# A hybrid attention, recurrence and MLP block on one core: the stretch from the output projection to the MLP, with token halves, a first half scaled by ScalarE and an order written out

## Chip, cores and metric

The kernel runs on one core of one Trainium2 chip. The metric is the device time in microseconds of one execution, as the median of several runs. A core has five engines with a queue each: PE (TensorE, matrix products), DVE (VectorE), ACT (ScalarE), POOL (GpSimd) and SP (SyncE, which here only issues DMAs). Each takes its own instructions strictly in the order of the built program and waits where a semaphore tells it to.

## What is computed

One layer on x of 1024 tokens by 1024 channels, in float32. Two branches (attention and a recurrence) give `merged`; the part that the change touches comes behind them:

```python
h = x.astype(f32) + merged @ w_out[layer].astype(f32)

hn = rmsnorm(h, norm2_g[layer])
a = jnp.square(jax.nn.relu(hn @ w_ff1[layer].astype(f32)))
h = h + a @ w_ff2[layer].astype(f32)
...
return rmsnorm(h, final_g).astype(x.dtype)
```

with `rmsnorm(x, g)` = x / sqrt(mean(x^2) + eps) * g, 1024 by 1024 for `w_out`, 1024 by 4096 for `w_ff1`.

## The kernel before

**Products.** A float32 product is made of three: each operand is split into a high part (a rounded copy, made by ACT, `hi_copy`, L142 in the profile) and a low part (the rest, a subtraction by DVE, `lo_sub`, L147). `three` issues high times high, low times high and high times low (L121). A "product" here has four steps of depth 128, so twelve matmuls of up to 512 columns into one PSUM bank. There are eight banks.

**Seven products instead of eight.** The projection, the MLP's first matrix (up) and its second (down) are each cut in two by two blocks and computed by a scheme of seven block products over sums of blocks. The names W, X, Y, V, Z are the banks of these products, and `LANDS` or the code of `out_start`, `out_rest`, `out_last` say with which sign each is added to which quadrant of the result.

**Projection** (`out_start`, `out_rest`, `out_last`). The token rows come in eight blocks of 128, `hres[0]` to `hres[7]`, called h in the profile. Blocks 0 to 3 are one half of the rows of the scheme and 4 to 7 the other. `out_start` computes W and X for four rows each; `out_rest(0..3)` computes Y from m1 and w1 (bank pwY), which two adds on DVE put into the right halves of h[tb] and h[4+tb]; `out_rest(4..7)` computes V from mb and w21 (pwV) for the left half of h[4+tb]; `out_last` computes Z from m4 and w22 (pwZ) for the right half of h[4+tb].

**Norm** (`norm2_token`). When a token block is complete, ACT squares it and sums along the row (L1451), POOL makes the factor in two small steps (L230 mean and eps, L233 power of -0.5, called n_ss and n_y), DVE multiplies block, factor and norm gain g2b (L1462, hn), and POOL issues a DMA that writes the block to DRAM (hd, L1467), from where the end of the kernel reads it back.

**Turning and forms** (`Quads`). PE turns hn by 128 by 128 transposes (L124) into banks hnt; ACT copies them to SBUF as hnq (L329). Quads holds two "halves" q = 0, 1 of the tokens for the MLP's scheme: before, q is the parity of the block (even and odd ones), so that each pair of blocks gives one transposed part of both. The operands of the seven up products are: 1 and 2, the q = 0 half itself; 6, 5, 7, 4, 3 sums of halves (made by DVE in `sums`, L347). Each form is split into sqh and sql.

**MLP up** (`UpPair`). 16 pairs, each of twice 128 columns of `w_ff1`; a pair has products 1 and 2 (bank pW), 6, 7, 4 (pX) and 5, 3 (pY), with its weights split as b11h/l, whiu/wlou and t0, t1 (sums of weight blocks). The first two pairs run ahead: their products 1 and 2 are cut here into two calls of 256 columns, the first of them while the last tokens are still normed. `mlp_up` then goes through the other pairs, with pair 2's first product inside it.

**MLP down and end** (`mlp_down`). Products pm over 32 steps; at the end blocks are normed once more and written out, even ones during the last group of steps, odd ones at its end.

**What sets the order.** A scheduler places the instructions of an engine by their dependencies and the order of the code. Where `after` adds a dependency without a semaphore, the order is fixed; `in_turn` does this for all of ACT's or DVE's instructions that go through it while `turns["on"]` is set. In the stretch of the change it is off before; `last_evac` orders some of ACT's.

Of the kernel before, what the change touches and what calls it, by code (L numbers as in the profile page):

```python
# [19 lines left out]
P = 128  # L20
# [19 lines left out]
def kernel(  # L40
# [94 lines left out]
    def in_turn(engine, ins):  # L135
        if turns["on"]:
            after(ins, turns[engine])
            turns[engine] = ins
        return ins

# [152 lines left out]
    class Quads:  # L293
# [3 lines left out]
        def __init__(self):  # L297
            self.raw, self.hl, self.s1 = {}, {}, []

# [4 lines left out]
        def fill(self, pr, src, name):  # L304


            banks = []
            for kp in range(KT // 2):
                if pr == 0:
                    for q in range(2):  # L310
                        self.raw[q, kp] = slot(f"{name}q{q}{kp}")
                pb = bank(f"{name}t{pr}{kp}")
                open_block("fill")
                for q in range(2):
                    for j in range(2):
                        kt, b = 2 * kp + j, 2 * q + j
                        transpose(
                            pb[:, b * P : (b + 1) * P],
                            src[2 * pr + q][:, kt * P : (kt + 1) * P],
                        )  # L320
                banks.append(pb)
                self.leave(pr, 0, kp, pb)
                self.split(1 + kp // 2, kp % 2, self.raw[0, kp], pr, 1)
            for kp in range(KT // 2):
                self.leave(pr, 1, kp, banks[kp])

        def leave(self, pr, q, kp, pb):
            last_evac[0] = after(
                nc.scalar.copy(  # L329
                    self.part(self.raw[q, kp], pr, 1),  # L330
                    pb[:, q * 256 : (q + 1) * 256].rearrange("p (k t) -> p k t", k=2),
                ),
                last_evac[0],
            )

        def split(self, i, kp, src, pr=0, n=4):
            if (i, kp) not in self.hl:
                self.hl[i, kp] = tuple(slot(f"sq{n_}{i}{kp}", F32R) for n_ in "hl")
            h, l = (self.part(t, pr, n) for t in self.hl[i, kp])
            self.last_lo = hi_lo(h, l, self.part(src, pr, n))  # L340

        def sums(self, pr, n, first=True, then=True):
            r = self.raw

            def tt(out, a, b, op):
                after(
                    nc.vector.tensor_tensor(  # L347
                        out=self.part(out, pr, n),
                        in0=self.part(a, pr, n),
                        in1=self.part(b, pr, n),  # L350
                        op=op,
                    ),
                    self.last_lo,
                )

            for kp in range(2):
                if pr == 0 and first:
                    self.s1.append(slot(f"sq1{kp}"))
                if first:
                    tt(self.s1[kp], r[1, kp], r[1, kp + 2], ALU.add)  # L360
                    tt(r[1, kp], r[0, kp], r[1, kp], ALU.subtract)
                    tt(r[0, kp], self.s1[kp], r[0, kp], ALU.subtract)
            for kp in range(2):
                if then:
                    tt(r[0, kp + 2], r[0, kp + 2], r[0, kp], ALU.subtract)

        def sum_form(self, i):
# [8 lines left out]
            for kp in range(2):  # L376
                self.split(i, kp, src[kp])

        def form(self, i, k, c0=0, n=512):
            h, l = self.hl[i, k // 2]  # L380
            c = (k % 2) * 512 + c0
            return h[:, c : c + n], l[:, c : c + n]
# [1056 lines left out]
    hsrc, hd = {}, {}  # L1439
# [3 lines left out]
    def norm2_token(tb):  # L1443
        hsrc[tb] = slot(f"hn{tb}")
        parts = 2 if tb == NT - 1 else 1
        cuts = [slice(i * D // parts, (i + 1) * D // parts) for i in range(parts)]
        sums = []
        for i, cs in enumerate(cuts):
            ssq = small.tile([P, 1], F32, tag="ssq1", name=f"n2_{tb}_ss{i}", bufs=4)
            after(  # L1450
                nc.scalar.activation(  # L1451
                    hsrc[tb][:, cs], hres[tb][:, cs], AF.Square, accum_out=ssq
                ),
                last_evac[0],
            )
# [3 lines left out]
        r = inv_rms(sums[0], 1, 1.0 / D, f"n2_{tb}")  # L1459
        yield  # L1460
        for cs in cuts:
            nc.vector.scalar_tensor_tensor(  # L1462
                out=hsrc[tb][:, cs], in0=hres[tb][:, cs], scalar=r, in1=g2b[0][:, cs],
                op0=ALU.mult, op1=ALU.mult,
            )
        hd[tb] = dram(f"hd{tb}", [P, D])
        nc.gpsimd.dma_start(hd[tb], hres[tb])  # L1467
# [7 lines left out]

    def out_operands(w=(), m=(), last=None):

        for n in w:
            src = tw[int(n)] if len(n) == 1 else out_block(int(n[0]) - 1, int(n[1]) - 1)
            out_form[n] = out_unit(n, src)  # L1480
            out_form[n].split()
        for n in m:
            merged[n] = []
            for kp in range(2):
                r = slot(f"m{n}r{kp}")
                h, l = slot(f"m{n}h{kp}", F32R), slot(f"m{n}l{kp}", F32R)
# [656 lines left out]
```

## Time and profile before

| What | us |
|---|---|
| median of 3 runs | 1462.3 |
| lowest and highest | 1461.54, 1463.45 |
| the profiled execution | 1462.87 |
| its span, first to last instruction | 1460.8 |

The stretch of the change lies between about 789 and 897 us of the span: the last twelve products of the projection, the norms and transposes, and the first products of the MLP. In rows of the timeline the columns are start, length, engine, line, operation, output<-inputs and shape; in brackets stands how long the engine sat idle before, and what ended that. A matmul's length (0.39 us at 512 columns) overlaps the next one's; they start 0.23 us apart.

### The profile page before, as it was taken

Reading aid. Unit: us, or ns where it says so; the run is one execution under the profiler, and the core shown is the slowest. Engines: PE = TensorE matmul, PEld = TensorE weight load, DVE = VectorE, ACT = ScalarE, POOL = GpSimd, SP = SyncE. Lnnn points to the kernel's source line nnn. Section 1 sums busy time; section 2 is a strip of 40 time slices with the busy share of each in tenths; the row PEclk is TensorE's granted clock in tenths of the full one; section 3 lists DMA queues with packets and bytes.
Section 4 is the critical chain, followed back from the end, with each engine's and each line's share of the span. In section 5 each row is a group of like instructions: output and inputs, shape, how many; then the busy total and the mean of one; then the engine's idle time right before and its main releaser. Section 6 shows DMA issues by size and latency. Waiting matters only on the chain.

```text
span 1460.8 us, 20051 instructions
## 1 busy us (share of the span) xinstructions
PE 1437.6 (98%) x7490; PEld 1224.0 (84%) x7490; DVE 1105.9 (76%) x1591; ACT 671.5 (46%) x1180; POOL 132.9 (9%) x319
## 2 busy tenths in 40 slices
PE   8999999999999999999999899999999999999997
PEld 8889988988898888888887788888888888888886
DVE  6699898698757787887777898666666757768765
ACT  7566666552323334423355464444444533523333
POOL 3021111000000012100011200000000000000041
PEclk9999999999999999999999999999999999999999
DMA  7143255001213349655489213444445975676734
GB/s 209 34 120 88 60 107 109 16 29 53 86 30 101 78 155 249 216 187 190 149 281 314 100 51 130 159 151 151 158 159 178 354 262 185 249 279 242 280 103 171
DMA packets 157736, 227.30 MB, mean 156 GB/s; under 512 B 25308, under 2 KB 92936, under 8 KB 157640
## 3 DMA queue, kind: packets, MB, share of 16 engines
q1 hardware_dynamic: 142664, 184.07, 37.2%
q0 software_dynamic: 11376, 35.40, 9.4%
q10 hardware_dynamic: 3600, 6.56, 1.2%
q8 instruction: 59, 0.97, 0.3%
q14 instruction: 37, 0.30, 0.1%
HBM read 163.34 MB, written 62.65 MB: 155 GB/s over the span
## 4 chain that ended last, share of the span: by engine, by line
PE 92%; DVE 4%; POOL 1%; issue 1%; DMA 1%; ACT 1%; SPq 0%; POOLq 0%; DVEq 0%; ACTq 0%
PE pm L121 18%; PE pX L121 9%; PE pY L121 6%; PE pW L121 6%; PE pjqk L121 6%; PE pjv L121 3%; PE pga L121 3%; PE pjq L121 3%; PE pys L121 3%; PE pyh L121 3%; PE gY L121 3%; PE gX L121 3%; PE pji L121 3%; PE pjf L121 3%; PE pjg L121 3%; PE po L121 3%
## 5 line engine op out<-in xcount | busy, mean ns | idle before, releaser
L142 ACT CAST whid<-w 128x1024 fp32r<-128x1024 f32 x31 | 32.6, 1053 | 153.6 <-PE pm L121 88.9
L679 DVE TENSOR_TENSOR_SCAN rm<-rm,bits 128x511 f32<-128x511 f32 (+7 forms) x72 | 87.2, 1219 | 14.4 <-ACT rm L657 12.8
L121 PE MATMUL pm<-wlod,sh 128*128 128x512 f32 x248 | 96.6, 390 | 1.0 <-DVE wlod L147 1.0
L121 PE MATMUL pm<-whid,sl 128*128 128x512 f32 x248 | 96.5, 389 | 0.0
L121 PE MATMUL pm<-whid,sh 128*128 128x512 f32 x248 | 96.5, 389 | 0.0
L147 DVE TENSOR_TENSOR wlod<-w,whid 128x1024 fp32r<-128x1024 f32 x31 | 37.9, 1223 | 58.3 <-ACT whid L142 58.3
L121 PE MATMUL pm<-th,sl 128*128 128x512 f32 x200 | 77.8, 389 | 0.0
L121 PE MATMUL pm<-tl,sh 128*128 128x512 f32 x200 | 77.8, 389 | 0.0
L121 PE MATMUL pm<-th,sh 128*128 128x512 f32 x200 | 77.8, 389 | 0.0
L147 DVE TENSOR_TENSOR sl<-sa,sh 128x1024 fp32r<-128x1024 f32 x56 | 68.2, 1219 | 1.4 <-ACT sh L142 1.4
L142 ACT CAST wTh<-pw 128x128 fp32r<-128x128 f32 (+3 forms) x96 | 44.4, 487 | 50.1 <-PE pw L124 45.2
L142 ACT CAST sh<-sa 128x1024 fp32r<-128x1024 f32 x56 | 57.2, 1046 | 12.1 <-DMA sa<-ad 12.1
L147 DVE TENSOR_TENSOR wTl<-pw,wTh 128x512 fp32r<-128x512 f32 (+3 forms) x96 | 50.7, 547 | 9.9 <-ACT wTh L142 5.4
L121 PEld LDWEIGHTS pm<-wlod,sh 128*128 128x128 f32 x248 | 46.5, 188 | 11.1 <-DVE wlod L147 1.4
L1809 POOL TENSOR_SCALAR fss<-fss 128x1 f32<-128x1 f32 x8 | 4.5, 561 | 563.0 <-ACT fsc L1804 562.5
L121 PEld LDWEIGHTS pm<-whid,sh 128*128 128x128 f32 x248 | 46.6, 188 | 9.8
L121 PEld LDWEIGHTS pm<-whid,sl 128*128 128x128 f32 x248 | 46.5, 187 | 9.6
L155 DVE TENSOR_TENSOR bt<-bt,rm 128x511 f32<-128x511 f32 (+7 forms) x72 | 49.0, 686 | 4.5 <-ACT bt L660 0.3
L657 ACT ACTIVATE rm<-z 128x511 f32<-128x511 f32 (+6 forms) x96 | 47.6, 503 | 5.2 <-DVE bt L155 1.9
L121 PE MATMUL pX<-sql,t1h 128*128 128x512 f32 x128 | 49.8, 389 | 0.0
L121 PE MATMUL pX<-sqh,t1h 128*128 128x512 f32 x128 | 49.8, 389 | 0.0
L121 PE MATMUL pX<-sqh,t1l 128*128 128x512 f32 x128 | 49.8, 389 | 0.0
(920 smaller groups left out, 4602.6 us busy)
## 6 DMA issues: line engine op xcount, KB each, us to landing
w<-in_w_ff_dram SPq DMA_DIRECT2D x72, 512.0 KB, 4.6
sa<-ad SPq DMA_DIRECT2D x56, 512.0 KB, 6.5
ad<-a SPq DMA_DIRECT2D x32, 256.0 KB, 4.1
ad<-s SPq DMA_DIRECT2D x16, 512.0 KB, 3.6
tw<-in_w_out_dram POOLq DMA_DIRECT2D x6, 1024.0 KB, 7.4
x<-in_x_dram SPq DMA_DIRECT2D x8, 512.0 KB, 9.5
xnl<-xnh POOLq DMA_DIRECT2D x8, 512.0 KB, 9.9
pr<-pd SPq DMA_DIRECT2D x8, 512.0 KB, 6.2
```

Of the source, the lines that this page charges most:

```text
L121: return pe(nc.tensor.matmul(*a, **k))
L142: return in_turn("act", nc.scalar.copy(dst, src))
L147: nc.vector.tensor_tensor(out=dst, in0=src, in1=hi.bitcast(F32), op=ALU.subtract),
L155: return nc.vector.tensor_tensor(out=out, in0=a, in1=b, op=ALU.mult)
L657: nc.scalar.activation(rm[:, s0 + c0 - 1 : s0 + m - 1], z[:, c0:m], AF.Sigmoid, scale=-0.125)
L679: sc = nc.vector.tensor_tensor_scan(out=rr, data0=rr, data1=bits[:, 1024 - nk + a : 1024 - nk + b][:, ::-1], initial=rm[:, b : b + 1] if i ...
L1809: nc.gpsimd.tensor_scalar(out=ssq, in0=ssq, scalar1=1.0 / D, scalar2=EPS, op0=ALU.mult, op1=ALU.add)
```

## The change

1. *Halves alike.* The MLP's two token halves are now blocks 0 to 3 and 4 to 7, as in the projection, instead of even and odd ones. The transposes of a half's pair of blocks fill four banks of their own (`turned`, `leave`), and `land`, `finish_tokens` and the last norms use the new numbers.
2. *First half scaled by ScalarE.* For blocks 0 to 3 ACT multiplies by the row's factor, and the norm gain, which after the transpose belongs to a partition, is put in when ACT copies out of PSUM. Blocks 4 to 7 stay with DVE.
3. *Last product onto the bank of the sum.* Y is added to h[tb] only; Z is accumulated onto Y's bank, and one add puts both into h[4+tb].
4. *First products among the norms.* Products 1 and 2 of the first two pairs are issued at the full 512 columns between the transposes of blocks 4 to 7, and product 1 of pair 2 behind them.
5. *Order written out.* From the first Y to the first `x7`, ACT's and DVE's instructions follow the code; loads of mb, w22 and m4 are separated from their splits; hd is issued behind the factors.

```diff
+        def leave(self, q, pr):
+            for kp, pb in self.banks.items():
+                if q == 0:
+                    for j in range(2):
+                        g = prm[:, G2 + 2 * kp + j : G2 + 2 * kp + j + 1]
+                        dst = self.part(self.raw[0, kp], 2 * pr, 2)[:, j]
+                        bs = slice(2 * j * P, 2 * (j + 1) * P)
+                        act(nc.scalar.activation(dst, pb[:, bs], AF.Identity, scale=g))
+                else:
+                    src = pb.rearrange("p (k t) -> p k t", k=2)
+                    act(nc.scalar.copy(self.part(self.raw[1, kp], 2 * pr, 2), src))
...
+    def norm2_scale(tb, parts=1):
+        n = D // parts
+        for i in range(parts):
+            cs = slice(i * n, (i + 1) * n)
+            if tb < 4:
+                scaled[tb] = act(
+                    nc.scalar.activation(
+                        hsrc[tb][:, cs], hres[tb][:, cs], AF.Identity, scale=rms[tb]
+                    )
+                )
+                continue
...
-            for h in (hres[tb][:, right], hres[4 + tb][:, right]):
-                turn_dve(add(h, h, oY[tb]))
...
+    def out_z(tb):
+        out_product(oY[tb], "4", "22", tb, False)
         h = hres[4 + tb][:, right]
-        turn_dve(add(h, h, Z))
+        dve(add(h, h, oY[tb]))
...
-            h = hres[2 * tb + int(q[0]) - 1]
+            h = hres[4 * (int(q[0]) - 1) + tb]
...
+    turns.update(on=True, act=None, dve=None)
     for tb in range(4):
+        out_y(tb)
+        if tb == 1:
+            merged_split("b")
+        norm2_sums(tb)
         if tb > 0:
+            norm2_scale(tb - 1)
+    first[0].sums()
+    out_v(0)
+    add_v(0)
+    out_v(1)
+    norm2_scale(3)
     for tb in range(4):
+        leave_h(tb, scaled[3])
+    merged_load("4")
+    add_v(1)
+    hn.turned(0, 0, hsrc, "hn")
+    hn.leave(0, 0)
+    out_operands(["22"])
+    out_v(2)
+    add_v(2)
+    merged_split("4")
+    out_v(3)
+    add_v(3)
+    hn.turned(0, 1, hsrc, "hn")
+    hn.leave(0, 1)
+    hn.first_hi(0)
+    hn.first_lo()
+    first[1].sums()
+    hn.first_hi(1)
+    out_z(0)
+    norm2_sums(4)
+    hn.first_lo(2)
+    out_z(1)
+    norm2_sums(5)
+    norm2_scale(4)
+    hn.first_lo(2)
+    leave_h(4, scaled[4])
     pairs[2].load()
+    out_z(2)
+    norm2_sums(6)
+    norm2_scale(5)
+    leave_h(5, scaled[5])
+    out_z(3)
+    norm2_sums(7, 2)
+    norm2_scale(6)
+    leave_h(6, scaled[6])
+    first[0].w1()
     for u in first:
+        u.sum_hi(1)
+        u.sum_lo(1)
+    norm2_scale(7, 2)
+    leave_h(7, scaled[7])
+    hn.turned(1, 0, hsrc, "hn")
+    hn.leave(1, 0)
+    for kp in range(2):
+        hn.sums(0, 2, kp)
+    first[0].w2()
+    pairs[2].split_first()
+    first[1].w1()
+    hn.turned(1, 1, hsrc, "hn")
...
+    first[1].w2()
+    pairs[2].w1()
```

The built program shows three places. On POOL, at the norms of the first blocks (hd are the blocks on their way to DRAM, n_ss and n_y the two steps of a factor), before:

```order
L1467 DMA hd_7908<-h_7487 128x1024
L1467 DMA hd_7932<-h_7488 128x1024
L1467 DMA hd_7956<-h_7489 128x1024
L1467 DMA hd_7973<-h_7490 128x1024
L230 TENSOR_SCALAR n_0_ss_7881<-n_0_ss_7881 128x1
L233 TENSOR_TENSOR n_0_y<-n_0_ss_7881,expo 128x1
```

and with the change, from the third block on:

```order
L236 TENSOR_SCALAR n_2_ss_7913<-n_2_ss_7913 128x1
L239 TENSOR_TENSOR n_2_y<-n_2_ss_7913,expo 128x1
L236 TENSOR_SCALAR n_3_ss_7934<-n_3_ss_7934 128x1
L239 TENSOR_TENSOR n_3_y<-n_3_ss_7934,expo 128x1
L1491 DMA hd_7972<-h_7487 128x1024
L1491 DMA hd_7974<-h_7488 128x1024
```

The four issues of hd moved from ahead of the four factors to behind them.

On ACT, from the first square sum to the first copy out of a transposed bank, before:

```order
L1451 ACTIVATE hn_7880,n_0_ss_7881<-h_7487 128x1024
L1451 ACTIVATE hn_7901,n_1_ss_7902<-h_7488 128x1024
L1451 ACTIVATE hn_7925,n_2_ss_7926<-h_7489 128x1024
L1451 ACTIVATE hn_7949,n_3_ss_7950<-h_7490 128x1024
L142 CAST m4h_7980<-m4r_7979 128x1024
L142 CAST m4h_7986<-m4r_7985 128x1024
L329 COPY hnq_8023<-hnt_8025 128x2x128
```

and with the change (mbh is the high part of mb; n_0_y as an input marks a scaling by the factor):

```order
L1465 ACTIVATE hn_7867,n_0_ss_7868<-h_7487 128x1024
L148 CAST mbh_7798<-mbr_7797 128x1024
L148 CAST mbh_7802<-mbr_7801 128x1024
L1465 ACTIVATE hn_7891,n_1_ss_7892<-h_7488 128x1024
L1477 ACTIVATE hn_7867<-h_7487,n_0_y 128x1024
L1465 ACTIVATE hn_7912,n_2_ss_7913<-h_7489 128x1024
L1477 ACTIVATE hn_7891<-h_7488,n_1_y 128x1024
L1465 ACTIVATE hn_7933,n_3_ss_7934<-h_7490 128x1024
L1477 ACTIVATE hn_7912<-h_7489,n_2_y 128x1024
L1477 ACTIVATE hn_7933<-h_7490,n_3_y 128x1024
L333 ACTIVATE hnq_7989<-hnt_7990,prm 128x256 x2
```

The four scalings came to ACT, each one square sum behind its own; mb's split moved in among them, and m4's behind the first copies.

On DVE, at the last product of the projection and the norms of blocks 4 to 6, before:

```order
L1072 TENSOR_TENSOR h_7491<-h_7491,pwZ_8135 128x512
L1072 TENSOR_TENSOR h_7492<-h_7492,pwZ_8158 128x512
L1462 SCALAR_TENSOR_TENSOR hn_8149<-h_7491,n_4_y,g2b 128x1024
L1462 SCALAR_TENSOR_TENSOR hn_8172<-h_7492,n_5_y,g2b 128x1024
L1072 TENSOR_TENSOR h_7493<-h_7493,pwZ_8181 128x512
L147 TENSOR_TENSOR sql_8032<-hnq_8023,sqh_8031 128x2x128
L1462 SCALAR_TENSOR_TENSOR hn_8195<-h_7493,n_6_y,g2b 128x1024
```

and with the change:

```order
L1087 TENSOR_TENSOR h_7491<-h_7491,pwY_7853 128x512
L153 TENSOR_TENSOR sql_8090<-hnq_7989,sqh_8089 128x2x256
L153 TENSOR_TENSOR sql_8093<-hnq_7995,sqh_8092 128x2x256
L1087 TENSOR_TENSOR h_7492<-h_7492,pwY_7873 128x512
L1483 SCALAR_TENSOR_TENSOR hn_8126<-h_7491,n_4_y,g2b 128x1024
L153 TENSOR_TENSOR sql_8096<-hnq_8001,sqh_8095 128x2x256
L153 TENSOR_TENSOR sql_8099<-hnq_8007,sqh_8098 128x2x256
L1087 TENSOR_TENSOR h_7493<-h_7493,pwY_7898 128x512
L1483 SCALAR_TENSOR_TENSOR hn_8147<-h_7492,n_5_y,g2b 128x1024
L1087 TENSOR_TENSOR h_7494<-h_7494,pwY_7919 128x512
L1483 SCALAR_TENSOR_TENSOR hn_8175<-h_7493,n_6_y,g2b 128x1024
```

The low parts of the first half, now 512 wide, stand between an add and the scaling of that block, and the scaling of block 4 stands behind the add of block 5.

More of the change, by code (lines that the diff above doesn't have):

```diff
@@ L298, in __init__ @@
             self.raw, self.hl, self.s1 = {}, {}, []
+            self.later = deque()
         @staticmethod
@@ L320, in fill @@
                         )
[L321 to L333, printed above, removed]
-            )
@@ L336, in split @@
[L336 to L342, printed above, removed]
-            r = self.raw
[L345 to L365, printed above, removed]
@@ L2061 @@
-    for tb in range(4, NT):
-        out_last(tb - 4)
-        if tb == NT - 1:
-            for u in first:
-                last_evac[0] = after(u.sum_hi(1), last_evac[0])
-            first[0].w1(0, 256)
-        side = norm2_token(tb)
-        next(side)
-        if tb == NT - 1:
-            hn.sums(2, 1, then=False)
-        if tb == 6:
-            hn.fill(2, hsrc, "hn")
-        for _ in side:
-            pass
-    pairs[2].load()
-    first[1].w1(0, 256)
-    first[0].w2(0, 256)
-    first[0].sum_lo(1)
@@ L2087 @@
-    hn.sums(3, 1, then=False)
-    hn.sum_form(6)
-    after(first[1].sum_lo(1), hn.last_lo)
+        u.sum_hi(0)
+        u.sum_lo(0)
+    for kp in range(2):
+        hn.next_sum(kp)
     for u in first:
         u.x6()
-    first[0].sum_split(0)
-    hn.sum_form(5)
-    first[1].sum_hi(0)
-    after(first[1].sum_lo(0), hn.last_lo)
+    hn.sum_form(7)
     for u in first:
         u.y5()
-    hn.sum_form(7)
+    for kp in range(2):
+        hn.last_sum(kp)
+    hn.sum_form(4)
+    turns["on"] = False
@@ L2099 @@
     for u in first:
         u.x7()
-    hn.sums(2, 2, first=False)
-    hn.sum_form(4)
     pairs[2].split()
```

294 lines of the change are left out of this document (158 added, 136 removed).

## The prediction

> **What bounds the kernel now.** The page first. PE is busy almost throughout, so time can only come from where PE waits or runs slow.
>
> ```profile
> span 1460.8 us, 20051 instructions
> PE 1437.6 (98%) x7490; PEld 1224.0 (84%) x7490; DVE 1105.9 (76%) x1591; ACT 671.5 (46%) x1180; POOL 132.9 (9%) x319
> ```
>
> The chain in order of time finds the place. Its columns are start, length, work.
>
> ```profile
> 789.24 10.89 PE pwY L121 x48
> 809.17 4.87 DVE hn L1462 x4
> 853.58 5.47 PE pX L121 x24
> 894.41 2.72 PE pW L121 x12
> 897.13 2.95 PE pX L121 x13
> ```
>
> A product is twelve 512-wide matmuls: 2.72 us (the pW row). From the first pwY (789.24) to pair 3's first pX (897.13) pass 107.9 us, and the chain leaves PE for DVE, POOL and ACT between. From 853.58 on it is PE again, sixteen products in 43.55 us, which is 16 x 2.72 with no loss. The PE timeline shows the waits in brackets, with what ended them:
>
> ```profile
> 803.24 0.51 PE L121 MATMUL pwV<-wout21h,mbl 128*128 128x512 f32 x1 [1.30 <-DVE mbl L147]
> 810.51 0.44 PE L124 MATMUL hnt<-ident,hn 128*128 128x128 f32 x2 [0.59 <-DVE hn L1462]
> 811.70 1.75 PE L124 MATMUL hnt<-ident,hn 128*128 128x128 f32 x14 [0.76 <-DVE hn L1462]
> 816.03 2.26 PE L124 MATMUL hnt<-ident,hn 128*128 128x128 f32 x16
> 829.10 0.41 PE L124 MATMUL hnt<-ident,hn 128*128 128x128 f32 x2 [2.60 <-DVE hn L1462]
> 831.01 3.25 PE L124 MATMUL hnt<-ident,hn 128*128 128x128 f32 x14 [1.50 <-DVE hn L1462]
> 838.15 0.28 PE L121 MATMUL pW<-sqh,b11h 128*128 128x256 f32 x1
> 838.27 0.28 PE L121 MATMUL pW<-sql,b11h 128*128 128x256 f32 x1
> 845.34 1.75 PE L124 MATMUL hnt<-ident,hn 128*128 128x128 f32 x14 [1.77 <-DVE hn L1462]
> ```
>
> The waits sum to 8.5 us. The other loss is the clock, third number from the end in the view by windows:
>
> ```profile
> core 0: us, PE busy (x) PEld busy (x) DVE busy (x) ACT busy (x) POOL busy (x), PEclk, DMA share, GB/s
> 810.00:815.00 5.00, 3.73 (x24) 3.21 (x25) 5.00 (x5) 2.64 (x8) 0.00 (x0) 1.00 0.00 0
> 830.00:835.00 5.00, 3.99 (x17) 3.79 (x18) 2.61 (x4) 3.26 (x10) 1.60 (x3) 0.51 0.55 187
> 835.00:840.00 5.00, 5.00 (x27) 4.35 (x26) 3.31 (x9) 3.38 (x8) 0.61 (x1) 0.81 0.97 285
> 818.00:898.00 80.00, 74.13 (x376) 63.38 (x375) 67.99 (x109) 47.90 (x90) 8.80 (x13) 0.96 0.28 102
> ```
>
> 0.49 x 3.99 + 0.19 x 5.00 = 2.9 us lost to the clock, right after the 2.60 and 1.50 us waits. Now the whole stretch: PE's own work is 12 products of the projection (32.6), 96 half-wide matmuls at 838.27 - 838.15 = 0.12 (11.5), 64 transposes at about 0.12 (sixteen start within 2.26 - 0.27; 7.7) and 43.5 behind 853.58: 95.3. So 107.9 - 95.3 = 12.6 are lost: 8.5 waits, 2.9 clock, 1.2 crumbs.
>
> **The change, part by part.** *Full width.* The first two pairs' pW go from 96 half-wide to 48 full matmuls, 10.9 us for 11.5: -0.6. Pair 2's first product only moves ahead. PE's work to the same point is then 32 x 2.72 + 7.7 = 94.7, so the most that this stretch can give is 107.9 - 94.7 = **13.2 us**.
>
> *Norms of the first half.* Why hn came at 809.17, although the square sums of the first tokens were ready long before, the timelines of ACT and POOL show:
>
> ```profile
> 795.93 0.19 ACT L1451 ACTIVATION_READ_ACCUMULATOR hn<-h 128x1 f32 x1
> 801.14 0.53 POOL L1467 DMA_DIRECT2D hd<-h  x1 [1.23 <-DVE h L1072]
> 801.74 0.35 POOL L230 TENSOR_SCALAR n_ss<-n_ss 128x1 f32<-128x1 f32 x1
> 802.18 1.43 POOL L233 TENSOR_TENSOR n_y<-n_ss,expo 128x1 f32<-128x1 f32 x1
> 805.05 0.56 POOL L233 TENSOR_TENSOR n_y<-n_ss,expo 128x1 f32<-128x1 f32 x1
> ```
>
> A square sum was there at 796.1; POOL's four issues of hd stood ahead of its two small steps, the last of them waiting for a DVE add until 801.14. Now they stand behind, so a norm costs its sum (1.06 + 0.19), two POOL steps (0.35 + 1.43 here) and a scaling. ScalarE's scaling from a per-token factor has no row in this width; the nearest:
>
> ```profile
> L1451 ACT ACTIVATE hn<-h 128x1024 f32<-128x1024 f32 x7 | 7.4, 1055 | 6.9 <-DVE h L1072 6.9
> L1823 ACT ACTIVATE y<-hb,fr x4: 722/722/725, 1447.7 to 1455.9; 128x512 f32<-128x512 f32 x4
> ```
>
> The full-width Square takes 1.06, two half-wide scalings from such a factor 1.44; I take 1.15, near the row of the same width. Four DVE scalings (4.87) and four of the eight adds of pwY (4 x 0.60) leave DVE. The scaling adds a wait on ACT for POOL: behind it stand the next token's square sum and later the first evacuation, which PE's third pwV waits for through its bank. Token 1's chain ends about 5.4 + 0.6 + 1.2 + 1.8 + 1.1, and 1 behind other ACT work, = 11 us after pwY begins; PE comes to its transposes after six products, 16.3. So 5 us of slack, and the 0.59 and 0.76 go. The 1.30 goes as well: b's low parts are due at 10.9, and with ACT's casts at 4.5 to 6.4 they are done near 9, since DVE has only eleven 512-wide and six 1024-wide instructions in this quarter, 13.4 us of 25.6 at the prices below.
>
> *The last operands.* The splits of w22 and m4 now follow the first evacuation on ACT: eight scaled 256-wide copies, then four casts. Nearest rows: scaled copies of the first norm, and plain ones here.
>
> ```profile
> L280 ACT ACTIVATE xnh<-xnt,prm x24: 465/502/731, 9.6 to 36.1; 128x256 fp32r<-128x256 f32 x16, 128x512 fp32r<-128x512 f32 x8
> L329 ACT COPY hnq<-hnt 128x256 f32<-128x256 f32 x32 | 10.6, 385 | 17.7 <-PE hnt L124 17.7
> ```
>
> Less 0.1 of overlap, 0.28 to 0.4 each: 2.3 to 3.2; I take 2.9. Then four casts as wide as that Square, 4 x 0.95, and DVE's 1.14 for the last low part: m4's low is whole about 9.6 after the transposes begin; the last product starts at 9.3 and needs that part 1.8 later. The four banks of pwY stay taken, so the third pwV waits for the first bank of transposes: two copies, done about 1.4 after the block began, which lasts 1.9. Zero for both, at most 1 us together. The loads of w22 and m4 keep their place in SP's queue; hd's four writes, later now, meet the idle DMA of the 810 row.
>
> *Second half.* Four norms remain on DVE, each waiting for POOL, and PE has a pair's first product (2.72) between the transposes. That covers most of the 2.60 + 1.50 + 1.77; with them goes the slow clock (2.9).
>
> *What is late next: DVE.* PE no longer gives it time. Count its order from the last pwV add to the low half of pair 3's sums, which pX of pair 3 waits for: 58 adds or splits 512 wide, 23 of 1024, 3 scalings of 1024 and 2 of 512. Prices are start to start:
>
> ```profile
> 894.45 0.69 DVE L1072 TENSOR_TENSOR a<-p,pX 128x512 f32<-128x512 f32 x1
> 895.17 0.69 DVE L1072 TENSOR_TENSOR a<-a,pY 128x512 f32<-128x512 f32 x1
> 895.77 1.22 DVE L147 TENSOR_TENSOR t1l<-w_3r,t1h 128x1024 fp32r<-128x1024 f32 x1
> ```
>
> The second starts 0.72 after the first, which it needs, the third 0.60 after the second: 0.69 less 0.09. So 0.60 and, of 1.22, 1.14; scalings 1.2 (809.17) and about 0.7. So 34.8 + 26.2 + 3.6 + 1.4 = 66.0 (before, 68.0 in 818 to 898, the windows row). PE has in that stretch 24 products and 32 transposes, 69.2. DVE may wait 3.2 us in all; what it waits beyond, PE waits. Before it waited:
>
> ```profile
> DVE hn L1462 <- POOL n_y L233: 4.6, 4, 2.4
> DVE sql L147 <- ACT sqh L142: 3.1, 3, 1.9
> DVE h L1072 <- PE pwZ L121: 1.7, 1, 1.7
> DVE t1l L147 <- ACT t1h L1648: 1.1, 1, 1.1
> DVE u L1072 <- PE pY L121: 0.8, 1, 0.8
> DVE wlou L147 <- ACT whiu L142: 0.3, 1, 0.3
> ```
>
> That is 11.6. Low end: only ten dependent neighbours at 0.12, 1.2, so nothing is given back. High end: all 11.6 again and these 1.2: 9.6 back. I take 8.3, nearer the upper end, since these norms still wait for POOL and the new order still puts low parts behind ACT's copies: 8.3 - 3.2 = **5.1 back**, as many short PE waits among the norms and up to pair 3.
>
> Beyond pair 3 the loops are the same, and so is the tail, where tokens only change names. Sum: 13.2 - 5.1 = 8.1. The profiled span 1460.8 becomes 1452.7; that execution took 1462.87, so 2.1 lie outside: 1454.8. It stood 0.57 above the median, hence **1454.2** for the median.
>
> **The rivals.**
> *A: DVE keeps up.* With waits of 1.2 to 3.2 in that stretch nothing comes back: all 13.2 are gained, 1449.1. The plain 0.56 step at 805.05 speaks for it, the 1.43 against.
> *B: the second half's norms stay late.* If one POOL answer slips by 2 us, as the 2.60 did, the transposes of tokens 4 and 5 wait, the clock drops again (2.9), and DVE's waits go to the upper end: 13.2 - 9.6 = 3.6 gained, the clock's loss lying in the same time: 1458.7. For it: POOL still issues hd between the norms. Against: DVE and PE have other work in between.
> *C: the relief is worth nothing.* What was taken from DVE early doesn't help if its later order decides alone; with 14 us of waits there, more than any row adds up to, 10.8 come back and 2.4 are left: 1459.9.
> *D: slower, through POOL.* Its small steps stretch while DVE works, once very far:
>
> ```profile
> 1419.98 4.65 POOL L1813 TENSOR_SCALAR fss<-fss,fss 128x1 f32<-128x1 f32 x1
> ```
>
> DVE waits in a written order, so if one step of each of four norms took 4.65 for 0.35, that is 17.2 us later: 1454.2 + 17.2 = 1471. It decides from 2 us per norm on. Against it: DVE itself stands still while it waits, which leaves POOL alone; 4.6 was the sum of four before. The Trainium skill, "SBUF — State Buffer", Who interferes with whom, has a VectorE instruction with two SBUF inputs contend with GpSimd reads. The trace agrees: 0.56 beside an add from PSUM, 1.43 beside a split.
>
> *E: transposes slow the clock.* PE now runs four blocks of sixteen, two of them beside norms. If one cost the clock as the 830 rows show, 2.9 us, the time is 1457.1. Between 809.9 and 813.4 PE ran transposes alone, with 1.35 of waits, and the 810 row has a clock of 1.00; the new blocks last 1.9 and a wait, so I give it little. The Trainium skill, "TensorE: Matmul & The Clock Gate", Part 4: PE-mode transpose, says that transposes do not count as busy in the same way, and by it E would be the likelier; the 810 row speaks against that, the 830 row fits either.
>
> **How the numbers follow.** Forecast 0.61, A 0.10, B 0.14, C 0.08, D 0.04, E 0.03. A measurement of this kernel tells about 0.2% (2.9 us) from no change. Faster are the forecast, A, B and E, 0.88; same C, 0.08; slower D, 0.04. The range goes from nearly all of A (0.4 back) to the upper end of what DVE gives back (9.6): 1449.5 to 1458.7. Outside lie part of A, C and D, under 0.2.
>
> **What would show it.** Right: one granted clock of 1.00 from 790 to 900; no PE wait for mbl or hn over 1 us; POOL's n_y of token 0 within 4 us of pwY's first add; afterwards short PE waits ended by DVE's sql, t1l or a, about 5 us in sum, with DVE over 90% busy. Wrong: a half clock behind the last product (B), PE waits on m4l, or DVE waits for n_y above 2 us each (D); no PE waits at all would be A.

## The result and the profile after

| | before | with the change |
|---|---|---|
| median, us | 1462.1 (4 runs, 1461.54 to 1463.45) | 1455.0 (4 runs, 1454.49 to 1455.19) |
| ratio to before, 95% interval | | 0.995 [0.9932, 0.9967] |
| the profiled execution, us | 1462.87 | 1454.49 |
| its span, us | 1460.8 | 1452.7 |

The change makes the kernel 0.5% shorter, and the interval does not reach 1. The page of the changed kernel: PE is at 99% in place of 98%, over a span 8.1 us shorter.

```profile
span 1452.7 us, 19895 instructions
PE 1436.7 (99%) x7442; PEld 1219.9 (84%) x7442; DVE 1096.7 (75%) x1557; ACT 675.6 (47%) x1166; POOL 125.2 (9%) x319
```

Where the 8.1 us lie is seen by three marks of the PE timeline: the first matmul of the first pwY, the first of pair 3's pX and the first of pm, with which the MLP's second matrix begins.

```profile
789.26 0.39 PE L121 MATMUL pwY<-wout1h,m1h 128*128 128x512 f32 x1
...
888.32 0.50 PE L121 MATMUL pX<-sqh,t1h 128*128 128x512 f32 x1
...
1139.89 0.39 PE L121 MATMUL pm<-whid,sh 128*128 128x512 f32 x1
```

The kernel before has the same marks here:

```profile
789.08 0.39 PE L121 MATMUL pwY<-wout1h,m1h 128*128 128x512 f32 x1
...
896.97 0.39 PE L121 MATMUL pX<-sqh,t1h 128*128 128x512 f32 x1
...
1147.20 0.39 PE L121 MATMUL pm<-whid,sh 128*128 128x512 f32 x1
```

From the first mark to the second 107.89 us became 99.06 (-8.8); to the third, 358.12 became 350.63 (-7.5): 1.3 us are lost again in and behind the pX of pair 3. Another 0.8 came off behind the third mark, and 0.2 were lost ahead of the first; together the 8.1. These are all waits of PE of 0.2 us or more from 785 to 905 us, in the timeline of the changed kernel:

```profile
829.37 1.86 PE L124 MATMUL hnt<-ident,hn 128*128 128x128 f32 x15 [0.64 <-DVE hn L1483]
856.21 0.50 PE L121 MATMUL pX<-sql,t0h 128*128 128x512 f32 x1 [0.23 <-DVE sql L153]
862.57 0.47 PE L121 MATMUL pX<-sqh,t1h 128*128 128x512 f32 x1 [0.85 <-DVE a L1087]
874.74 0.49 PE L121 MATMUL pX<-sqh,t1l 128*128 128x512 f32 x1 [0.52 <-DVE t1l L153]
889.68 0.50 PE L121 MATMUL pX<-sqh,t1l 128*128 128x512 f32 x1 [0.64 <-DVE t1l L153]
```

The waits of 1.30 for mbl, of 2.60, 1.50 and 1.77 for hn are gone; five short ones are left, 2.9 us in sum, and four of them stand behind the norms. The windows show the clock (third number from the end) at 1.00 where it had been 0.51:

```profile
789.00:814.00 25.00, 25.00 (x126) 21.06 (x124) 15.35 (x20) 19.11 (x29) 6.17 (x12) 1.00 0.53 204
830.00:835.00 5.00, 4.98 (x28) 4.10 (x27) 4.11 (x4) 5.00 (x10) 2.90 (x6) 1.00 0.52 207
814.00:889.50 75.50, 72.51 (x329) 57.62 (x327) 68.96 (x88) 48.48 (x77) 6.60 (x13) 1.00 0.29 108
```

In the first 25 us DVE (the third pair of numbers) is busy 15.35, in the 75.5 us behind them 68.96. What it waits for in that second stretch, in the view of waits (us in sum, times, longest):

```profile
DVE sql L153 <- ACT sqh L148: 2.3, 2, 1.4
DVE t1l L153 <- ACT t1h L1685: 1.8, 2, 1.1
DVE u L1087 <- PE pY L121: 1.2, 1, 1.2
DVE hn L1483 <- POOL n_y L239: 0.7, 2, 0.3
DVE wlou L153 <- ACT whiu L148: 0.2, 1, 0.2
```

That is 6.2 us, and for the rest of that stretch DVE is at work. From 846.92 to 867.09 it runs without a wait, and the PE waits of 0.23 and 0.85 end on it there: in that part DVE is the engine that is late. POOL's second step for the first factor starts 5.2 us after pwY begins (before, 13.1), and hd is issued behind the fourth:

```profile
794.15 0.19 POOL L236 TENSOR_SCALAR n_ss<-n_ss 128x1 f32<-128x1 f32 x1 [30.56 <-ACT hn L1465]
794.42 0.57 POOL L239 TENSOR_TENSOR n_y<-n_ss,expo 128x1 f32<-128x1 f32 x1
...
803.45 2.21 POOL L1491 DMA_DIRECT2D hd<-h  x4
```

### The profile page after: what moved, and what is told of

Its sections match the earlier page's. It is cut to its first block, busy times and chain, and to the rows that moved or that the text cites. A ratio compares the mean times of both kernels' runs of the same rounds, so it can differ in the third digit from the quotient of the medians.

```text
span 1452.7 us, 19895 instructions
## 1 busy us (share of the span) xinstructions
PE 1436.7 (99%) x7442; PEld 1219.9 (84%) x7442; DVE 1096.7 (75%) x1557; ACT 675.6 (47%) x1166; POOL 125.2 (9%) x319
## 5 line engine op out<-in xcount | busy, mean ns | idle before, releaser
L148 ACT CAST wTh<-pw 128x128 fp32r<-128x128 f32 (+3 forms) x96 | 44.3, 486 | 50.0 <-PE pw L124 45.2
```

The lines of the kernel that those rows point to most:

```text
L148: return in_turn("act", nc.scalar.copy(dst, src))
```

## The experiments

The theory to test is that of the prediction: early factors and relieved DVE bring the first norms in time, products among the norms cover the second ones and keep the clock, and DVE's lateness gives part of it back. Each run was timed beside the kernel before (medians 1462.0 to 1462.2). An interval of the ratio is 2.6 to 5 us wide, so among the shorter runs a difference of 1 or 2 us is not shown by the medians alone. The last column is read from the trace of one execution, from the first pwY to the first pm as above; it leaves out what differs ahead of that stretch and behind it: the start of pwY alone lies between 788.7 and 790.5 us in the runs made from the changed kernel.

| Run | median, us | ratio to before | pwY to pm, us |
|---|---|---|---|
| before | 1462.1 | | 358.1 |
| the change | 1455.0 | 0.995 [0.9932, 0.9967] | 350.6 |
| f5, no products among the norms | 1463.9 | 1.001 [1.0001, 1.0019] | 359.2 |
| h3, the first product only | 1460.4 | 0.9988 [0.9979, 0.9997] | 356.0 |
| f6, pair 2's product in the loop | 1455.2 | 0.9955 [0.9943, 0.9968] | 351.1 |
| f9, DVE scales, own bank for Z | 1454.1 | 0.9945 [0.9932, 0.9957] | 349.7 |
| f3, hd ahead of the factors | 1458.0 | 0.9971 [0.996, 0.9982] | 353.3 |
| f4, before with hd behind | 1461.6 | 0.9996 [0.9987, 1.0005] | 358.2 |
| e1, weight sums early | 1453.9 | 0.9943 [0.993, 0.9955] | 348.7 |
| e2, these and more early | 1455.0 | 0.9951 [0.9938, 0.9963] | 350.3 |
| e3, 2.3 us more on DVE | 1458.6 | 0.9975 [0.9965, 0.9985] | 355.2 |
| e4, 4.6 us less on DVE | 1454.4 | 0.9946 [0.9934, 0.9959] | 349.3 |
| h1, order free | 1452.6 | 0.9937 [0.9925, 0.995] | 348.5 |
| h5, f9 with sums early | 1453.5 | 0.994 [0.9927, 0.9954] | 348.9 |

### Which part carries the gain: f5, h3, f6

f5 takes the first products out from among the norms and leaves all else:

```diff
-    first[0].w1()
     for u in first:
         u.sum_hi(1)
...
-    first[0].w2()
     pairs[2].split_first()
-    first[1].w1()
     hn.turned(1, 1, hsrc, "hn")
     hn.leave(1, 1)
+    first[0].w1()
+    first[0].w2()
+    first[1].w1()
```

> The changed kernel, with the first products of the first two pairs issued behind all transposes of the second half, not among them. Theory (they cover the norms of blocks 4 to 7): PE stands before the transposes of blocks 5 and 7 for 2.5 to 4 us each, ended by DVE hn, as before the change, and the clock falls behind them; 7 to 10 us longer than the changed kernel, so at or above the time of the kernel before. Rival (the written order alone brings the second half's norms in time): no wait for hn above 1 us, 0 to 2 us longer. Second rival (DVE is the bound to pair 3 whatever PE does, so PE's waits only move ahead and those behind vanish): 2 to 4 us longer.

8.9 us longer than the change, so the whole gain is gone; the run is 1.8 us longer than before. Its PE timeline has the waits for hn again:

```profile
827.67 0.30 PE L124 MATMUL hnt<-ident,hn 128*128 128x128 f32 x1 [0.54 <-DVE hn L1483]
830.58 3.49 PE L124 MATMUL hnt<-ident,hn 128*128 128x128 f32 x16 [2.61 <-DVE hn L1483]
836.00 2.39 PE L124 MATMUL hnt<-ident,hn 128*128 128x128 f32 x15 [1.93 <-DVE hn L1483]
```

and its windows the clock:

```profile
830.00:835.00 5.00, 3.49 (x16) 3.09 (x16) 4.50 (x5) 4.91 (x11) 4.11 (x7) 0.66 0.45 184
835.00:840.00 5.00, 4.00 (x20) 3.37 (x21) 4.93 (x9) 3.52 (x7) 0.16 (x1) 0.76 0.27 108
840.00:845.00 5.00, 4.33 (x17) 3.21 (x16) 3.48 (x6) 0.58 (x1) 0.00 (x0) 0.89 0.00 0
```

The three waits are 5.1 us, two of 0.67 at the second half of pW (for ACT's copy of its first) 1.3; less the 0.64 and 0.23 that the change has, 5.5. The clock costs 0.34 x 3.49 + 0.24 x 4.00 + 0.11 x 4.33 = 2.6. Together 8.1 of the 8.5 us between the marks. The norms themselves come when they come with the change. In f5 DVE scales blocks 4 and 7 here:

```profile
826.24 1.29 DVE L1483 SCALAR_TENSOR_TENSOR hn<-h,n_y,g2b 128x1024 f32<-128x1024 f32 x1 [0.34 <-POOL n_y L239]
...
835.20 1.40 DVE L1483 SCALAR_TENSOR_TENSOR hn<-h,n_y,g2b 128x512 f32<-128x512 f32 x2
```

and with the change block 4 here:

```profile
825.03 1.29 DVE L1483 SCALAR_TENSOR_TENSOR hn<-h,n_y,g2b 128x1024 f32<-128x1024 f32 x1 [0.34 <-POOL n_y L239]
```

Counted from the first pwY the scalings of blocks 4 and 7 start at 35.8 and 44.7 us in f5, at 35.8 and 45.2 with the change (block 7 at 834.45), and at 38.6 and 55.5 in the kernel before (827.67 and 844.53). So the norms of the second half are earlier than before, and that alone brings nothing: PE is there earlier still, and what the change adds is that it has other work meanwhile. The first theory holds (the third wait is shorter than it said), both rivals fall. No run has the full-width products among the norms without halves alike: they need the first half of the tokens whole, so what f5 shows is the worth of parts 1 and 4 together.

h3 leaves product 1 of the first pair where the change put it and moves the other two behind:

```diff
-    first[0].w2()
     pairs[2].split_first()
-    first[1].w1()
     hn.turned(1, 1, hsrc, "hn")
     hn.leave(1, 1)
+    first[0].w2()
+    first[1].w1()
```

> The changed kernel with one of the three products left among the norms: product 1 of the first pair stays ahead of the transposes of blocks 4 and 5; product 2 of that pair and product 1 of the next go behind the transposes of blocks 6 and 7. The run without any of them lost 8.9 us against the changed kernel: waits for hn of 0.54, 2.61 and 1.93 and two half-clock spells. Theory (each product covers the norm behind it, and the clock falls only where two long waits come close together): the wait of 2.61 shrinks to about 0.6, one wait of 3 to 4 us for hn of block 7 stays, the clock stays at 1.00; 2.5 to 4.5 us longer than the changed kernel. Rival (one wait of 3 us or more halves the clock): 4.5 to 7 us longer. Second rival (DVE, the bound behind, takes the wait as its own rest): 0 to 2 us longer.

5.4 us longer than the change: the first rival. The wait behind the product that stayed is 0.64, as in the change; the others for hn are 0.37 (block 6) and, 0.3 us behind it, 3.33 (block 7), and the clock fell right behind them:

```profile
835.33 3.46 PE L124 MATMUL hnt<-ident,hn 128*128 128x128 f32 x15 [3.33 <-DVE hn L1483]
```

```profile
835.00:840.00 5.00, 4.67 (x21) 4.44 (x22) 4.93 (x9) 2.98 (x6) 0.00 (x0) 0.66 0.02 5
```

0.34 x 4.67 = 1.6 us of clock. I had taken one wait of 3 us for harmless; here, with the short one ahead of it, it was not. The 8.9 us so divide into 3.5 for the first product and 5.4 for the other two.

f6 puts pair 2's first product, which the change issues ahead of the sums of halves, back into the loop:

```diff
     first[1].w2()
-    pairs[2].w1()
...
             o.y3()
+        u.w1()
         u.x6()
```

> The changed kernel with product 1 of the third pair back in the loop behind the first two pairs. Theory (DVE is the bound to pair 3, so where PE waits doesn't matter): PE waits 2 to 3 us for sqh and sql at the first pX, and the waits behind it go; within 1 us of the changed kernel. Rival (that product covers the first sums of halves): 1.5 to 3 us longer. Second rival (waits of 1.9 and 1.1 us in a row halve the clock): 3 to 5 us longer.

0.2 us longer, as the theory had it. PE waits where that product had been, and the clock falls even here:

```profile
842.65 0.49 PE L121 MATMUL pX<-sqh,t1h 128*128 128x512 f32 x1 [1.56 <-ACT sqh L148]
844.03 0.80 PE L121 MATMUL pX<-sql,t1h 128*128 128x512 f32 x1 [0.89 <-DVE sql L153]
```

```profile
840.00:845.00 5.00, 2.55 (x8) 1.58 (x7) 4.93 (x7) 3.13 (x5) 0.00 (x0) 0.89 0.00 0
845.00:850.00 5.00, 5.00 (x19) 3.96 (x18) 4.13 (x5) 3.87 (x5) 0.00 (x0) 0.77 0.13 52
```

2.45 us of waits and 0.11 x 2.55 + 0.23 x 5.00 = 1.4 of clock; the later waits of 0.23, 0.85, 0.52 and 0.64, and the slow starts beside them, are all gone. Two things lie in this. DVE's first add of a product 3 (u), which waits for PE, starts here in f6:

```profile
867.87 0.69 DVE L1087 TENSOR_TENSOR u<-u,pY 128x512 f32<-128x512 f32 x1 [1.15 <-PE pY L121]
```

and here with the change:

```profile
868.33 0.69 DVE L1087 TENSOR_TENSOR u<-u,pY 128x512 f32<-128x512 f32 x1 [1.24 <-PE pY L121]
```

Behind the first pwY these are 79.0 us in f6 and 79.1 with the change, although PE has done one product less by then in f6: up to there DVE sets the time, and it does not matter where PE waits for it, not even whether PE runs at half speed meanwhile. Behind that add the product stands in the loop where the change waits for t1l, and covers those waits instead.

### What the parts on DVE, ACT and POOL are worth: f9, f3, f4

f9 undoes the scaling by ScalarE and the shared bank; DVE gets 7.3 us more.

```diff
-            if tb < 4:
-                scaled[tb] = act(...)
-                continue
...
-        h = hres[tb][:, right]
-        dve(add(h, h, oY[tb]))
+        for h in (hres[tb][:, right], hres[4 + tb][:, right]):
+            dve(add(h, h, oY[tb]))
...
-        out_product(oY[tb], "4", "22", tb, False)
+        Z = bank(f"pwZ{tb}")
+        out_product(Z, "4", "22", tb, True)
```

> The changed kernel with two parts undone: blocks 0 to 3 are scaled by DVE again (with the gain, and plain copies out of the banks), and Z has its own bank, with Y added to both halves by DVE; order otherwise as written. DVE gets four scalings (4.9 us) and four adds (2.4 us) more, all of them ahead of the last pwV add. Theory (DVE has room there: busy 15.35 of 25 us in the first quarter; the two parts bring nothing by themselves): within 1 us of the changed kernel, either sign. Rival (what DVE does there makes it late all the way to pair 3): 3 to 7 us longer, with longer PE waits ended by sql and a.

0.9 us shorter than the change, if anything. Its windows, as those of the change above:

```profile
789.00:814.00 25.00, 25.00 (x129) 21.19 (x127) 23.17 (x28) 13.56 (x22) 7.94 (x12) 1.00 0.51 195
814.00:889.50 75.50, 73.03 (x329) 58.18 (x328) 69.02 (x88) 47.82 (x73) 6.60 (x13) 1.00 0.29 108
```

DVE takes the 7.3 us as 23.17 - 15.35 = 7.8 busy in the first window, where PE loses nothing, and in the second DVE is busy as long as with the change. Parts 2 and 3 bring nothing here. They have a price on ACT: eight scaled copies out of the transposed banks take 3.04 us, the four plain ones of f9 2.06. In f9 the low parts of the first half start 1.0 us earlier behind pwY, and PE's wait of 0.64 for hn is gone; that the one brings the other is likely, but not tested alone.

f3 puts POOL's issues of hd back ahead of the factors (with ACT's scalings behind the square sums, so that they don't block them):

```diff
         norm2_sums(tb)
-        if tb > 0:
-            norm2_scale(tb - 1)
+        last_hd = leave_h(tb, last_hd)
+    for tb in range(4):
...
+        norm2_scale(tb)
```

> The changed kernel with POOL's four issues of hd for blocks 0 to 3 ahead of the four factors again, and ACT's four scalings behind the four square sums. Theory (the first step of the prediction: factors then come only after the last add of pwY): first n_y near 12.5 us after pwY begins in place of 5, PE waits for the first transposes and for the third pwV about 1 us each, 1 to 3.5 us longer than the changed kernel. Rival (the slack of 5 us covers it): within 0.7 us. Second rival (two waits so close halve the clock): 4 to 6 us longer.

3.0 us longer than the change, inside the theory's range. The four factors wait for the fourth issue, as before the change. But POOL made all four first steps ahead of the second ones, so the first n_y starts 15.0 us behind pwY and not 12.5 as expected (before, 13.1), and the 3.0 are somewhat more than the issues alone cost. The last factor is done at 806:

```profile
800.96 0.53 POOL L1494 DMA_DIRECT2D hd<-h  x1 [2.04 <-DVE h L1087]
801.56 2.21 POOL L2088 TENSOR_SCALAR n_ss<-n_ss 128x1 f32<-128x1 f32 x4
803.85 2.13 POOL L2093 TENSOR_TENSOR n_y<-n_ss,expo 128x1 f32<-128x1 f32 x4
```

PE waits for it, 1.9 us in three pieces:

```profile
805.65 0.33 PE L124 MATMUL hnt<-ident,hn 128*128 128x128 f32 x1 [0.28 <-ACT hn L1480]
806.69 1.86 PE L124 MATMUL hnt<-ident,hn 128*128 128x128 f32 x15 [0.71 <-ACT hn L1480]
809.49 0.50 PE L121 MATMUL pwV<-wout21h,mbh 128*128 128x512 f32 x1 [0.94 <-ACT hnq L333]
```

f4 makes the same step in the kernel before, alone:

```diff
             next(sides[3], None)
+            for i in range(4):
+                hd[i] = dram(f"hd{i}", [P, D])
+                after(nc.gpsimd.dma_start(hd[i], hres[i]), last_n[0])
```

> The kernel before, with one thing of the change: hd of blocks 0 to 3 is issued behind the four factors (and behind DVE's fourth scaling). Theory (POOL made hn late, as the prediction has it): n_y of block 0 comes 5 us earlier, the first scaling with it, the PE waits of 0.59 and 0.76 go; 1.5 to 3 us shorter than before. Rival (DVE made it late: it runs without a pause from 801.4 to 818 and its scalings stand behind ten other instructions in its order, so an earlier factor only waits): within 0.7 us of before, first scaling again near 20 us after pwY begins.

The rival: 0.5 us shorter, an interval across 1. POOL has the first factor 5 us earlier, and DVE's scalings begin when they did:

```profile
797.26 1.43 POOL L233 TENSOR_TENSOR n_y<-n_ss,expo 128x1 f32<-128x1 f32 x1
```

```profile
808.33 0.69 DVE L1075 TENSOR_TENSOR w_1r<-w_1r,w_1r 128x512 f32<-128x512 f32 x1
808.94 4.87 DVE L1463 SCALAR_TENSOR_TENSOR hn<-h,n_y,g2b 128x1024 f32<-128x1024 f32 x4
```

PE waits for them as long as before (0.58, 0.76, 2.60 and so on). The scaling starts as soon as DVE is through with the weight sum ahead of it, without a bracket: the factor had been there for 10 us.

### What DVE's work is worth behind the norms: e1 to e4, h1, h5

e1 moves the four weight sums of the second pair from behind the low parts of the first half to ahead of the first transposes:

```diff
     add_v(1)
+    first[1].sums()
     hn.turned(0, 0, hsrc, "hn")
...
     hn.first_lo()
-    first[1].sums()
```

> The changed kernel with one edit: the four DVE subtractions for pair 1's weight sums (4 x 0.60 and 0.12 for each dependent neighbour, 2.8 us) move from the busy stretch behind the last pwV add to the place of the second pwV add, where DVE stood idle 3.8 us. Theory (DVE's order behind the last pwV add is what PE waits for): 1.5 to 2.8 us less than the changed kernel's 1455.0, so about 1452.8, and the PE waits between 825 and 890 us shorter. Rival (those waits are set by ACT or POOL, or by products themselves): within 0.7 us of 1455.0.

1.9 us less between the marks, as the theory has it; 1.1 by the medians, short of its range. The wait of 0.64 for hn is gone, that of 0.23 for sql falls below 0.15, those for a and t1l stay. e2 moves them further ahead, and the splits of both pairs' t1 with them:

```diff
     norm2_scale(3)
+    first[1].sums()
...
     add_v(1)
+    for u in first:
+        u.sum_hi(1)
+        u.sum_lo(1)
```

> As e1, and the splits of both pairs' t1 (two casts on ACT, two subtractions of 1.14 on DVE) move into the same idle place; pair 1's subtractions stand ahead of the second pwV add. Theory: DVE's stretch loses 5.1 us instead of 2.8, so up to 1 us more than e1 if nothing else is late; but the two casts (1.9 us) now stand ahead of the copies out of the first transposes on ACT, and through them delay the last operands m4, which had about 1 us of slack: so between 1451.5 and 1454.5. Rival (ACT sets the pace in this quarter): not better than e1, with a PE wait in front of the third pwV or the last product.

No gain is left, as the rival had it: PE waits 0.78 in the transposes of blocks 0 and 1 (for DVE's second pwV add, which stands behind the weight sums) and 0.62 ahead of the third pwV (for ACT's copies out of the bank, which stand behind the casts). Work put where an engine has room still delays what stands right behind it.

e3 makes one step of the sums of halves twice (2.3 us more on DVE), e4 leaves this step and the last one out (4.6 less):

```diff
     for kp in range(2):
         hn.next_sum(kp)
+        hn.next_sum(kp)
```

> The changed kernel with the two 1024-wide DVE subtractions of next_sum made twice: 2 x 1.14 = 2.3 us more work for DVE just before the operands of product 7, the same values. Theory (DVE is the bound there): one to one, +2.0 to +2.5 us, 1457.2. Rival (DVE has slack, PE waits for ACT): 0 to +0.7.

```diff
-    for kp in range(2):
-        hn.next_sum(kp)
...
-    for kp in range(2):
-        hn.last_sum(kp)
```

> The changed kernel without next_sum and last_sum: four 1024-wide DVE subtractions (4.5 us) are left out, so products 7 and 3 use operands that are not summed and the output is another one. Theory: the PE waits between 850 and 890 (0.23, 0.85, 0.52, 0.64 and some slow weight loads) go for the most part, -1.5 to -3.0 us, 1452.8; not -4.5, since PE has no more waits to give there. Rival: no change, within 0.7.

e3 cost 3.6 by the medians, more than the work put in; two waits close together halved the clock behind them:

```profile
857.17 0.47 PE L121 MATMUL pX<-sqh,t0h 128*128 128x512 f32 x1 [1.33 <-DVE u L1087]
858.81 0.50 PE L121 MATMUL pX<-sql,t0h 128*128 128x512 f32 x1 [1.17 <-DVE sql L153]
```

```profile
860.00:865.00 5.00, 5.00 (x17) 3.93 (x16) 5.00 (x5) 1.04 (x1) 0.00 (x0) 0.66 0.00 0
```

0.34 x 5.00 = 1.7 us of clock. Without it DVE's 2.3 came through as 1.9 by the medians and 2.9 between the marks (4.6 in all there), so about one to one. e4 gave 0.6 by the medians and 1.4 between the marks, a miss below the range expected: 0.23 and 0.85 went, the two waits for t1l stayed at 0.53 and 0.64. The first of these hangs on a chain (a weight sum on DVE, the high part on ACT, the low part on DVE), in which DVE waits 1.11 us for ACT in e4 as with the change. The second t1l starts right behind its neighbour on DVE, in both runs. So DVE is the bound there by little: more work costs its whole time, less gives only what the chain leaves.

h1 leaves out the written order of ACT and DVE:

```diff
-    turns.update(on=True, act=None, dve=None)
```

> The changed kernel without the written order of ACT and DVE in this stretch (the ordering dependencies are left out; the scheduler places their instructions from the same code). Theory (the written order is what keeps the scalings ahead of other DVE work; the scheduler had put ten instructions ahead of them before): PE waits for hn of the second half above 1 us come back, 3 to 8 us longer than the changed kernel. Rival (halves alike and the products among the norms do it, whoever orders): within 1 us, with waits of up to 1 us moved among sql and t1l.

The theory falls, and the result lies beyond the rival too: 2.4 us shorter than the change, the shortest of all runs (1452.21 to 1453.82 in 5 runs, against 1454.49 to 1455.19; the intervals of the two ratios overlap, the runs do not). Its DVE timeline shows a difference that accounts for most of it:

```profile
794.25 0.68 DVE L1090 TENSOR_TENSOR w_1r<-w_1r 128x512 f32<-128x512 f32 x1
...
796.89 0.69 DVE L1090 TENSOR_TENSOR w_1r<-w_1r 128x512 f32<-128x512 f32 x1
...
822.38 1.29 DVE L1483 SCALAR_TENSOR_TENSOR hn<-h,n_y,g2b 128x1024 f32<-128x1024 f32 x1
```

The scheduler put the weight sums of the second pair at 794 to 797, into the first window where DVE has room; in the written order they stand at 819 to 822. Block 4 is scaled at 822.38, in the change at 825.03, and no PE wait for hn is left. e1, which makes the same sums early in the written order, comes to 348.7 us between the marks against 348.5 here; by the medians it is 1.2 longer, so whether the order holds more than these sums is open. h5 combines f9 with the weight sums ahead of the second turned block:

```diff
     add_v(3)
+    first[1].sums()
     hn.turned(0, 1, hsrc, "hn")
```

> A version meant to be shorter: the run with DVE scaling and own bank for Z, and the second pair's four weight sums moved from behind the low parts of the first half to ahead of the transposes of blocks 2 and 3, where DVE is not the bound. Theory (DVE's work in the stage behind counts): the waits for hn at 829 and for sql go, those for a and t1l (0.85, 0.5, 0.6) stay; 1 to 2.5 us shorter than the changed kernel. Rival (nothing beyond what the run with own bank has): 1454.1, within 0.5 us of it.

1.5 us shorter than the change, inside the theory's range, and 0.6 shorter than f9, just outside the rival's; the single runs of the two overlap (1452.25 to 1455.50 and 1453.28 to 1454.93). Of the two waits that were to go, that for hn is gone in f9 already, and that of 0.23 for sql stays. It can't be told from e1 either.

## Why the prediction was right, and where not

*The sum.* Forecast were a span of 1452.7 and a median of 1454.2; measured were 1452.7 and 1455.0, 0.8 above. The signs named for it came: a clock of 1.00 from 790 to 900, no PE wait for mbl or hn over 1 us, the first factor within 4 us of pwY's first add, later short waits ended by sql, a and t1l. DVE is busy for 91% of the second stretch. The waits sum to 2.9 with hn and not 5: of the 4.4 us lost up to the mark at pair 3 the four waits ahead of it are 2.2, the other 2.1 slower matmul starts beside waits. That the span was met to a tenth is luck: between the first mark and pm the change gave 7.5 of the 8.1, and a tail 0.8 shorter, which was not forecast, made up the rest (0.2 were lost ahead of the first mark).

*The second half's norms.* Right, and larger than put: f5 shows that the whole net gain hangs on the products that stand among them (with part 1, which they need), with the clock (2.6 of it).

*DVE as the engine that is late.* Right in its sum, by luck: two errors cancel. From the last pwV add (at 815.38) to the end of t1l of pair 3 (889.6) pass 74.2 us; forecast were 66.0 of work and 8.3 of waits, 74.3. Measured waits are 6.2, so what was not waiting is 68.0: 2.0 more than my count, of which the low end's dependent neighbours would make 1.2. And the waits are other ones: POOL's part fell from 4.6 to 0.7, while I had kept it as the reason for the upper end; ACT's high parts (sqh, t1h, whiu) make 4.3. Given back to the mark at pair 3 are 13.2 - 8.8 = 4.4, with the 1.3 lost in and behind that pX 5.7, forecast 5.1. f6 shows that DVE sets the time up to the first product 3, e4 that 4.6 us less work there gives only 0.6 to 1.4.

*Norms of the first half.* Here a step was wrong. "Why hn came at 809.17": I read POOL's four issues of hd as the cause. f4 shows that they were not; the scaling stood behind other work in DVE's own order, and an earlier factor changed nothing. The trace of before had it: DVE runs from 801.36 to 809.17 without a bracket, and a scaling that waits for POOL would have one:

```profile
808.56 0.69 DVE L1075 TENSOR_TENSOR w_1r<-w_1r,w_1r 128x512 f32<-128x512 f32 x1
809.17 4.87 DVE L1462 SCALAR_TENSOR_TENSOR hn<-h,n_y,g2b 128x1024 f32<-128x1024 f32 x4
```

The waits of 0.59 and 0.76 went all the same, since the change also took the scalings out from behind that work. With the changed order the factors do matter (f3, at most 3.0 us), since the first scaling is asked for at 797. The second step, that four scalings and four adds leave DVE, was rightly outside the stage that is late, and f9 shows its worth as nothing.

*b's low parts and the last operands.* Zero waits for both, as costed.

*The tail.* Forecast as the same, it was 0.8 shorter. In the kernel before, PE waits 1.00 us for a low part at 1442; f4, whose code there is the same, waits 0.20 at 1441. So this differs between runs of one code, and is not shown to be the change.

*The rivals.* A (DVE keeps up) and B (half clock) did not come; f5 and h3 are what B describes, at 8.9 and 5.4 us in place of 4.5. C, that relief early on DVE is worth nothing, was right about the scalings and adds (f9) but not about the time, since the gain came from PE. D did not come: DVE's longest wait for a factor is 0.3 us. E, transposes that slow the clock, was not seen: the 830 to 835 window, which begins in a block of sixteen behind the 0.64 wait, is at 1.00.

## What to carry to other kernels

When an engine's wait names a producer, look first whether the waiting instruction has a bracket of its own: one that starts right behind its neighbour was held by the order, and a faster producer gains nothing. Here independent products of PE covered the late operands (f5, 8.9 us), while taking work from the engine that makes them, ahead of them, brought nothing (f9); and the cover was worth more than the waits it filled, since the clock stayed up. Where an order is written by hand, hold it against the scheduler's: here the change came with a written order that cost 2.4 us by the medians, 2.1 between the marks.

## What the runs showed of the hardware

*Waits that halve the clock.* A window of 5 us at 0.66 lacks 1.7 us of clock, which is half the clock for 3.4 us; in e3 the matmuls of such a spell start 0.43 us apart in place of 0.23. Such a spell followed 2.50 us of PE waits within 3 us (e3), 2.45 within 3 (f6, there across two windows) and 3.70 in two waits 0.3 us apart (h3); after 1.93 in three waits within 4.1 us (f3), and after the single 1.77 before the change, none came. In f5 a first spell followed 3.15 in two waits within 3.5 us, and a second one a wait of 1.93 alone that began 3.5 us behind these. The Trainium skill, "TensorE: Matmul & The Clock Gate", Part 1, has the clock set by windows of about 3.4 us that run on their own, and a rule against idle gaps above that. The spells' length agrees. The rule is not enough here: in e3, f6 and f5 spells came behind gaps that were each shorter, and in e3 and f6 gaps of 0.9 to 1.6 us seem to add up when they fall together. What decides it is not shown, since 1.93 us brought a spell once and once none.

*Where it costs nothing.* In f6 PE ran at 0.77 for 5 us, and the kernel was within 0.2 us of the change (0.4 between the marks): the slow clock cost nothing where DVE set the time.
